# Score products of even and odd heads issued in alternation into two PSUM banks, and a compression in blocks of 64 columns

## The chip, the core and the metric

One core of a Trainium2 chip (trn2) runs the whole program. The metric is the device time of one execution in microseconds (us). Five engines matter: TensorE (PE; its weight loads are shown as PEld), VectorE (DVE), ScalarE (ACT), GpSimd (POOL) and SyncE (SP), which issues the transfers.

## What is computed

Two blocks of two layers each on x of 256 x 1024 in float32. A layer of the first block is FFN, mixer, FFN; one of the second is mixer, FFN. Only the mixers are touched. Cut to what matters:

```python
# first mixer: 12 dilated heads in 3 groups share one softmax per query; 4 stick-breaking heads
s = einsum('bhrnqd,bhrnkd->bhrnqk', qb, kw) * 64 ** -0.5
...
z = einsum('bhqd,bhkd->bhqk', q_blk, k) * 64 ** -0.5
...
# second mixer: keys are compressed in blocks of 32 at stride 16 by an MLP, for K and for V
blk = swapaxes(k[:, idx], 2, 3) + pos
k_cmp = gelu(blk.reshape(bsz, n_cmp, g, 32 * 64) @ w1) @ w2
...
# 8 query heads over 2 key heads: attention to the compressed keys,
# to selected blocks and to a window of 512 (at 256 positions both are plain causal attention),
# and a fourth branch with a window of 128 and a sink
s = einsum("bqgrd,bkgd->bgrqk", qb, kb) * 64 ** -0.5
```

Head size is 64 everywhere, so a score product contracts 64 rows.

## The kernel before, in words

The 256 positions are two tiles t = 0, 1 of 128 rows. Linear layers run on PE with each operand split into a high and a low part (type fp32r): three products per tile (`mm3`, lines 184 to 186, or `lin_T`, `lin_T2`), with weights that `chunk` (line 104) loads by SP, and ACT (line 110, `wh`) and DVE (line 111, `wl`) convert, six buffers deep. PSUM has 8 banks: a pool `lin` of 4 for linear products and a pool `aux` of 4 for everything else. A scheduler places the instructions of each engine in a fixed order from the priorities of the code; it mixes linear products in between the steps of the attentions.

`attend1` (line 398) is the attention of the first mixer. `QT[t]` holds q and k transposed, two heads on top of each other: even heads in partitions 0 to 63, odd ones in 64 to 127 (`qk`, line 421). For each j of 4 the three heads j, 4 + j, 8 + j (one per group, so all of one parity) get their mask by a product with the identity (line 434) and their scores (line 440) in one aux bank at t = 0 and two at t = 1; then follow the maximum (line 442), the exponential (451), transposes (`transposed`, line 152), the copy to SBUF and the products with v (468). The stick-breaking heads take one bank per parity (lines 477 and 483).

`attn` (line 525) is called three times per tile in the second mixer, once with a window and sinks and twice causal. `scores(h0)` takes 4 heads of one parity at t = 0, 2 at t = 1, in one bank: mask (538 to 542), scores (546), maximum (549), exponentials (558). `output` transposes and multiplies by v (572). At most AHEAD = 2 score groups wait for their output. All groups of even heads come first, then those of odd heads:

```python
        for par in range(2):
            for h0 in range(par, 8, 2 * per):
                ahead.append(scores(h0))
```

The scores against the compressed keys (line 829) also go parity by parity. In `compress` (line 704) 16 slices of the blocks are the held operand, 32 columns wide (15 blocks and one of zeros for each of 2 key heads), split into `ah` and `al`; three products per slice go into 32 rows of one aux bank `hps` (lines 723 to 725), 16 slices for K and 16 for V. After the last linear product that follows, `hr` takes the GELU (749), is transposed (752), copied (754), multiplied by w2 for K (757), copied four ways by POOL (764) and multiplied by w2 for V (768).

On DVE a convolution of 31 taps (lines 863 and 866, 120 steps of line 866 a layer) fills the gaps of the second mixer.

Of the kernel before, what the change touches and what calls it, by code (L numbers as in the profile page):

```python
# [25 lines left out]
def body(tc, ctx, I, C, out, upto=99):  # L26
# [371 lines left out]
    def attend1(qkn, vs):  # L398
        QT = [None, None]
        oTs = []  # L400
        for t in range(2):
# [26 lines left out]
            for j in range(4):  # L428
                groups = [[0, 1, 2]] if t == 0 else [[0, 1], [2]]
                ps_l, mx, sm = [], stat(4), stat(4)  # L430
                for gi, gs in enumerate(groups):
                    n = len(gs) * nk * P
                    ps = aux_ps()[:, :n]
                    nc.tensor.matmul(ps, identb, dilm[t][:, gs[0]:gs[-1] + 1, :].rearrange("p g k -> p (g k)"),
                                     start=True, stop=False)
# [6 lines left out]
                    V.tensor_reduce(mx[:, gi:gi + 1], ps, op=OP.max, axis=AX.X)  # L442
                    ps_l.append(ps)
# [26 lines left out]

            n = nk * 256
            e2 = big("b", "se")
            zs, es, ws = [], blocks2(e2, n), []
            for par in range(2):
                o = par * 64
                z = aux_ps()[:, :n]
                nc.tensor.matmul(z[:, n - 256:], identb, sbm[:, None, :].to_broadcast([P, 2, P]), start=True, stop=False)
                for kt in range(nk):
                    for jj in range(2):
# [3 lines left out]
                        nc.tensor.matmul(z[:, c0:c0 + P], k_, q_, start=False, stop=(kt == nk - 1 and jj == 1))  # L483
                S.activation(es[par], z, AF.Abs)
                zs.append(z)
# [39 lines left out]
    def attn(t, qT, kTf, vf, window, sink=None):  # L525
# [5 lines left out]
        def scores(h0):  # L531
            par = h0 % 2
            hs = list(range(h0, h0 + 2 * per, 2))
            n = per * nk * P
            ps = aux_ps()[:, :n]
            pv = ps.rearrange("p (h k) -> p h k", h=per)
            if t == 0:
                nc.tensor.matmul(pv, identb, swm[:, None, P:].to_broadcast([P, per, P]), start=True, stop=False)
            elif window:
                nc.tensor.matmul(pv, identb, swm[:, None, :].to_broadcast([P, per, 2 * P]), start=True, stop=False)  # L540
            else:
                nc.tensor.matmul(pv[:, :, P:], identb, swm[:, None, P:].to_broadcast([P, per, P]), start=True, stop=False)
# [5 lines left out]
            sl = slice(h0, h0 + 2 * per - 1, 2)  # L548
            V.tensor_reduce(mx[:, sl], pv, op=OP.max, axis=AX.X)
            if sink is None:  # L550
                V.tensor_scalar(ng[:, sl], mx[:, sl], -0.125, None, op0=OP.mult)
            else:
                V.scalar_tensor_tensor(mx[:, sl], mx[:, sl], 0.125, sink[:, sl], op0=OP.mult, op1=OP.max)
                V.tensor_scalar(ng[:, sl], mx[:, sl], -1.0, None, op0=OP.mult)
            e = unit("e")[:, :n]
            ev = e.rearrange("p (h k) -> p h k", h=per)
            for i, h in enumerate(hs):
# [597 lines left out]
```

## Time and profile before

| | |
|---|---|
| median of 3 runs | 2174.1 us (2173.64 to 2177.4) |
| the profiled execution | 2173.62 us, span 2171.8 us |
| PE busy | 2142.1 us, 99% |
| weight loads (PEld) busy | 1824.8 us, 84% |
| DVE busy | 1567.7 us, 72% |
| ACT busy | 1159.0 us, 53% |
| POOL busy | 38.7 us, 2% |
| granted TensorE clock, mean | 0.998 |

The busy time of PE is that of pipelined products with modelled ends: the duration of one is not what it costs. Each float32 product of two operands appears as two records, a transpose or an fp32r product as one.

### The profile page before, as it was taken

To read this page: it belongs to the slowest core of one execution; us is meant where nothing else is said; L and a number is where in the kernel's file an instruction comes from. 1 tells how busy PE (TensorE), PEld (TensorE's weight loads), DVE (VectorE), ACT (ScalarE), POOL (GpSimd) and SP (SyncE) were. 2 spreads that over 40 slices of the span, in tenths; PEclk is the share of its full clock that TensorE was granted. 3 is DMA by queue.
4 is the path that set the end of the run, shared out by engine and by line. 5 is a ranking of instruction groups with operands and counts; after the bars stand their busy time and mean duration, and the time that the engine had idled before them with its cause. 6 is when DMAs were issued, how large, how long until landed. Compare 5 with 4: busy or idle time off the path is not lost.

```text
span 2171.8 us, 30964 instructions
## 1 busy us (share of the span) xinstructions
PE 2142.1 (99%) x11824; PEld 1824.8 (84%) x11824; DVE 1567.7 (72%) x2395; ACT 1159.0 (53%) x1766; POOL 38.7 (2%) x55
## 2 busy tenths in 40 slices
PE   7999999999999999999999999999999999999998
PEld 6888888888888888888887888889987888888997
DVE  6875556786677555577757997678976898577983
ACT  5654545554555455555545554456655554446652
POOL 0000000000000000000000000000000000000000
PEclk9999999999999999999999999999999999999999
DMA  8666534666666654366666632456656643355653
GB/s 252 202 193 186 193 97 139 192 192 190 192 188 187 188 191 127 118 183 185 190 188 198 200 117 78 155 172 200 192 188 191 216 140 113 107 184 175 186 179 121
DMA packets 250821, 373.86 MB, mean 172 GB/s; under 512 B 14768, under 2 KB 123696, under 8 KB 250672
## 3 DMA queue, kind: packets, MB, share of 16 engines
q1 hardware_dynamic: 250096, 371.48, 55.8%
q8 instruction: 93, 1.52, 0.3%
q0 software_dynamic: 576, 0.39, 0.1%
q14 instruction: 56, 0.46, 0.1%
HBM read 371.17 MB, written 1.05 MB: 171 GB/s over the span
## 4 chain that ended last, share of the span: by engine, by line
PE 93%; DVE 3%; issue 1%; DMA 1%; ACT 1%; POOL 1%; SPq 0%; POOLq 0%; DVEq 0%; ACTq 0%
PE lin L186 17%; PE lin L184 17%; PE lin L185 16%; PE lin L218 15%; PE lin L219 8%; PE aux L155 4%; PE lin L206 3%; PE lin L205 3%; PE lin L204 3%; PE aux L546 2%; PE aux L572 1%; DVE wl L111 1%; PE aux L440 1%; PE aux L468 1%; ACT wh L110 0%
## 5 line engine op out<-in xcount | busy, mean ns | idle before, releaser
L111 DVE TENSOR_TENSOR wl<-raw,wh 128x1024 fp32r<-128x1024 f32 (+1 forms) x688 | 835.1, 1217 | 407.5 <-ACT wh L110 399.8
L110 ACT ACTIVATE wh<-raw 128x1024 fp32r<-128x1024 f32 (+1 forms) x688 | 723.2, 1055 | 557.0 <-PE lin L186 314.1
L218 PE MATMUL lin<-x,wh 128*128 128x512 f32 x1408 | 494.9, 396 | 0.0
L219 PE MATMUL lin<-x,wl 128*128 128x256 f32 x1408 | 395.3, 281 | 0.0
L184 PE MATMUL lin<-wh,x 128*128 128x512 f32 (+2 forms) x896 | 350.0, 391 | 0.0
L185 PE MATMUL lin<-wl,x 128*128 128x512 f32 (+2 forms) x896 | 348.2, 389 | 1.5 <-DVE wl L111 1.5
L186 PE MATMUL lin<-wh,x 128*128 128x512 f32 (+2 forms) x896 | 348.2, 389 | 1.0 <-DVE rs L1057 0.8
L218 PEld LDWEIGHTS lin<-x,wh 128*128 128x128 f32 x1408 | 264.5, 188 | 61.6
L219 PEld LDWEIGHTS lin<-x,wl 128*128 128x128 f32 x1408 | 266.4, 189 | 0.5 <-DVE wl L111 0.4
L186 PEld LDWEIGHTS lin<-wh,x 128*128 128x128 f32 x896 | 168.9, 189 | 34.5 <-DVE rs L1057 1.6
L185 PEld LDWEIGHTS lin<-wl,x 128*128 128x128 f32 x896 | 168.9, 189 | 33.0 <-DVE wl L111 1.9
L184 PEld LDWEIGHTS lin<-wh,x 128*128 128x128 f32 x896 | 168.8, 189 | 32.6 <-ACT wh L110 0.4
L186 PE MATMUL lin<-wh,lo 128*128 128x512 f32 x480 | 188.6, 393 | 0.4 <-DVE lo L147 0.4
L184 PE MATMUL lin<-wh,hi 128*128 128x512 f32 x480 | 187.2, 390 | 0.0
L185 PE MATMUL lin<-wl,hi 128*128 128x512 f32 x480 | 187.0, 390 | 0.0
L205 PE MATMUL lin<-x,wh 128*128 128x256 f32 x576 | 163.2, 283 | 0.0
L206 PE MATMUL lin<-x,wl 128*128 128x256 f32 x576 | 163.0, 283 | 0.0
L204 PE MATMUL lin<-x,wh 128*128 128x256 f32 x576 | 163.0, 283 | 0.0
L205 PEld LDWEIGHTS lin<-x,wh 128*128 128x128 f32 x576 | 110.6, 192 | 0.1
L204 PEld LDWEIGHTS lin<-x,wh 128*128 128x128 f32 x576 | 110.6, 192 | 0.1
L206 PEld LDWEIGHTS lin<-x,wl 128*128 128x128 f32 x576 | 110.6, 192 | 0.0
L186 PEld LDWEIGHTS lin<-wh,lo 128*128 128x128 f32 x480 | 90.1, 188 | 19.5 <-DVE lo L147 1.3
(317 smaller groups left out, 2774.0 us busy)
## 6 DMA issues: line engine op xcount, KB each, us to landing
raw<-in_ffn_w_up_dram SPq DMA_DIRECT2D x168, 512.0 KB, 4.3
raw<-in_ffn_w_down_dram SPq DMA_DIRECT2D x132, 512.0 KB, 4.2
raw<-in_w_in_dram SPq DMA_DIRECT2D x132, 512.0 KB, 4.1
raw<-in_ffn_w_gate_dram SPq DMA_DIRECT2D x88, 512.0 KB, 4.4
raw<-in_w_gate_dram SPq DMA_DIRECT2D x64, 512.0 KB, 3.8
raw<-in_w_branch_dram SPq DMA_DIRECT2D x32, 512.0 KB, 4.4
raw<-in_w_out_dram SPq DMA_DIRECT2D x16, 512.0 KB, 4.4
raw<-in_nsa_cmp_w_dram SPq DMA_DIRECT2D x16, 512.0 KB, 4.3
```

What stands on the lines that cost most here:

```text
L110: S.activation(wh, raw, AF.Copy)
L111: V.tensor_sub(wl, raw, wh.bitcast(F32))
L155: nc.tensor.transpose(p[:, i * P:(i + 1) * P], s, ident)
L184: nc.tensor.matmul(ps, xt.h[k], w[0], start=start, stop=False)
L185: nc.tensor.matmul(ps, xt.h[k], w[1], start=False, stop=False)
L186: nc.tensor.matmul(ps, xt.l[k], w[0], start=False, stop=stop)
L204: nc.tensor.matmul(o, wh, xh, start=k == 0 and i % 2 == 0, stop=False)
L205: nc.tensor.matmul(o, wh, xl, start=False, stop=False)
L206: nc.tensor.matmul(o, wl, xh, start=False, stop=k == 7 and i % 2 == 1)
L218: nc.tensor.matmul(o, wh, x, start=k == 0, stop=False)
L219: nc.tensor.matmul(o[:, :T], wl, x[:, :T], start=False, stop=k == 7)
L546: nc.tensor.matmul(pv[:, i, kt * P:(kt + 1) * P], q_, kTf(kt, h), start=False, stop=(i == per - 1 and kt == nk - 1))
```

## The change

Everywhere that scores of even and odd heads were computed one parity after the other, a step now takes two groups of opposite parity, with a bank of its own for each, and issues their products in turn. `attend1` takes j = 0 and 1 together, then 2 and 3:

```diff
-            for j in range(4):
-                groups = [[0, 1, 2]] if t == 0 else [[0, 1], [2]]
-                ps_l, mx, sm = [], stat(4), stat(4)
+            def scores(js):
+                r = [([], stat(4), stat(4)) for _ in js]
                 for gi, gs in enumerate(groups):
                     n = len(gs) * nk * P
-                    ps = aux_ps()[:, :n]
...
+                    pss = [aux_ps()[:, :n] for _ in js]
+                    for ps in pss:
+                        nc.tensor.matmul(ps, identb, dilm[t][:, gs[0]:gs[-1] + 1, :].rearrange("p g k -> p (g k)"),
+                                         start=True, stop=False)
                     for gg in gs:
-                        h = gg * 4 + j
                         for kt in range(nk):
                             c0 = ((gg - gs[0]) * nk + kt) * P
-                            nc.tensor.matmul(ps[:, c0:c0 + P], qk(h, False, t), qk(h, True, kt), start=False,
-                                             stop=(gg == gs[-1] and kt == nk - 1))
+                            for ps, j in zip(pss, js):
+                                h = gg * 4 + j
+                                nc.tensor.matmul(ps[:, c0:c0 + P], qk(h, False, t), qk(h, True, kt), start=False,
+                                                 stop=(gg == gs[-1] and kt == nk - 1))
...
+            for js in ((0, 1), (2, 3)):
+                for j, r in zip(js, scores(js)):
+                    output(j, *r)
```

The stick-breaking scores and those against the compressed keys are turned round in the same way. In `attn` one call of `scores` makes both parities, and the loop over groups follows:

```diff
-            for i, h in enumerate(hs):
-                q_ = qT[par * 64:par * 64 + 64, (h // 2) * P:(h // 2 + 1) * P]
+            for i in range(per):
                 for kt in range(nk):
-                    nc.tensor.matmul(pv[:, i, kt * P:(kt + 1) * P], q_, kTf(kt, h), start=False,
-                                     stop=(i == per - 1 and kt == nk - 1))
+                    for par, pv in enumerate(pvs):
+                        h = h0 + 2 * i + par
+                        q_ = qT[par * 64:par * 64 + 64, (h // 2) * P:(h // 2 + 1) * P]
+                        nc.tensor.matmul(pv[:, i, kt * P:(kt + 1) * P], q_, kTf(kt, h), start=False,
+                                         stop=(i == per - 1 and kt == nk - 1))
...
-        for par in range(2):
-            for h0 in range(par, 8, 2 * per):
-                ahead.append(scores(h0))
-                if po is None:
-                    po = aux_ps()
-                if len(ahead) > AHEAD:
-                    output(*ahead.pop(0))
+        for h0 in range(0, 8, 2 * per):
+            ahead += scores(h0)
+            if po is None:
+                po = aux_ps()
+            while len(ahead) > AHEAD:
+                output(*ahead.pop(0))
```

The compression holds the high and the low part of a slice side by side, 64 columns, and needs two products: rows 0 to 31 of the result hold what the high part gives, rows 32 to 63 what the low part gives (this adds the product of the two low parts). They are added after the transpose, the GELU comes behind that, and the four copies of POOL become four GELUs on ACT. All this stands after the rotary step of the first tile instead of before both:

```diff
-            ah, al = unit("cAh", F32R), unit("cAl", F32R)
-            split(A, ah, al)
+            ahl = []
+            for q in range(2):
+                x = unit("cAh", F32R)
+                v = x.rearrange("p (s a n) -> p s a n", s=8, a=2)
+                split(A[:, q * 256:(q + 1) * 256].rearrange("p (s n) -> p s n", s=8), v[:, :, 0], v[:, :, 1])
+                ahl += [x[:, i * 64:(i + 1) * 64] for i in range(8)]
...
-                    nc.tensor.matmul(o, ah[:, a], ws[i][0], start=s == 0, stop=False)
-                    nc.tensor.matmul(o, ah[:, a], ws[i][1], start=False, stop=False)
-                    nc.tensor.matmul(o, al[:, a], ws[i][0], start=False, stop=s == 15)
+                    nc.tensor.matmul(o, ahl[s], ws[i][0], start=s == 0, stop=False)
+                    nc.tensor.matmul(o, ahl[s], ws[i][1], start=False, stop=s == 15)
...
-        hr = unit("hr")[0:32, :]
-        S.activation(hr, hps, AF.Gelu_apprx_tanh)
...
+                S.activation(hg4, h4[:, :, 1], AF.Copy)
+                V.tensor_tensor(hg4, h4[:, :, 0], hg4, op=OP.add)
+                hk = hg[:, 0:64]
...
+                        S.activation(hv5[:, hf, a], hg[:, 64 + hf * 32:96 + hf * 32].rearrange("p (g n) -> p g n", g=2)
+                                     [:, :, None, :].to_broadcast([P, 2, 2, 16]), AF.Gelu_apprx_tanh)
+                S.activation(hk, hk, AF.Gelu_apprx_tanh)
```

How this moves PE's instructions is seen in three places. A row is line, operation, written tile, read tiles and shape; `aux_` with a number is one tile of the aux pool. First the causal attention of the second mixer at t = 1, before:

```order
L542 LDWEIGHTS identb
L542 MATMUL aux_11449<-swm,identb 128x2x128
L546 MATMUL aux_11449<-kT_10823,qT_11408 128x128
L546 MATMUL aux_11449<-kT_10843,qT_11408 128x128
L546 MATMUL aux_11449<-kT_10823,qT_11408 128x128
L546 MATMUL aux_11449<-kT_10843,qT_11408 128x128
L542 LDWEIGHTS identb
L542 MATMUL aux_11461<-swm,identb 128x2x128
L546 MATMUL aux_11461<-kT_10823,qT_11408 128x128
```

And the same place now:

```order
L556 MATMUL aux_11446<-swm,identb 128x2x128
L556 LDWEIGHTS identb
L556 MATMUL aux_11448<-swm,identb 128x2x128
L563 MATMUL aux_11446<-kT_10773,qT_11382 128x128
L563 MATMUL aux_11448<-kT_10773,qT_11382 128x128
...
L563 MATMUL aux_11448<-kT_10809,qT_11382 128x128
L184 MATMUL lin_12038<-wh_12016,x_9761 128x512
L185 MATMUL lin_12038<-wl_12017,x_9761 128x512
L186 MATMUL lin_12038<-wh_12016,x_9761 128x512
L155 MATMUL aux_11468<-ident,e_11437 128x128 x4
```

Groups of 4 products into one bank have become runs of 8 that change the bank with every product; three linear products stand between the second such run and the first transpose of the exponentials.

Second the first mixer at t = 1, where a pair of heads takes four aux tiles, now:

```order
L444 MATMUL aux_2553<-qt_2523,qt_2522 128x128
L444 MATMUL aux_2554<-qt_2523,qt_2522 128x128
L437 LDWEIGHTS identb
L437 MATMUL aux_2567<-dilm_86,identb 128x256
L437 LDWEIGHTS identb
L437 MATMUL aux_2568<-dilm_86,identb 128x256
L444 MATMUL aux_2567<-qt_2357,qt_2522 128x128
L444 MATMUL aux_2568<-qt_2357,qt_2522 128x128
L444 MATMUL aux_2567<-qt_2523,qt_2522 128x128
L444 MATMUL aux_2568<-qt_2523,qt_2522 128x128
L185 MATMUL lin_2892<-wl_2845,x_1607 128x512
```

Nine linear products follow before the transposes of the exponentials; before the change a single head's two tiles stood there.

Third the place behind the compression, before:

```order
L752 MATMUL aux_10793<-ident,hr_10791 128x32 x4
L184 MATMUL lin_10878<-wh_10856,x_9761 128x512
L185 MATMUL lin_10878<-wl_10857,x_9761 128x512
...
L184 MATMUL lin_10878<-wh_10862,x_9761 128x512
L757 MATMUL aux_10800<-hg_10798,w_10472 128x32 x2
L768 MATMUL aux_10809<-w_10472,hv_10804 128x64 x2
L185 MATMUL lin_10878<-wl_10863,x_9761 128x512
```

And now, from the transposes of hr on (20 linear products, all but one left out here, follow them):

```order
L786 MATMUL aux_10786<-ident,hr_10784 128x64 x4
L186 MATMUL lin_10852<-wh_10842,x_9996 128x512
...
L155 MATMUL aux_10810<-ident,kd_10800 128x128 x4
L155 MATMUL aux_10816<-ident,dd_10801 128x128 x2
L804 MATMUL aux_10820<-hg_10791,w_10472 128x32 x2
L809 MATMUL aux_10824<-w_10472,hv_10792 128x64 x2
```

The two small products stood 7 linear products behind the transposes of hr, one behind the other; now they stand 20 linear products and six transposes behind them.

## Rows read from the trace of the kernel before

**Rows 1.** The page: span; busy time of PE; shares of the last chain by engine.
```profile
span 2171.8 us, 30964 instructions
...
PE 2142.1 (99%) x11824; PEld 1824.8 (84%) x11824; DVE 1567.7 (72%) x2395; ACT 1159.0 (53%) x1766; POOL 38.7 (2%) x55
...
PE 93%; DVE 3%; issue 1%; DMA 1%; ACT 1%; POOL 1%; SPq 0%; POOLq 0%; DVEq 0%; ACTq 0%
```

**Rows 2.** Groups of PE by form: line, tiles, shape, count | busy us, mean ns | idle before.
```profile
L572 PE MATMUL aux<-vv,pt 128*128 128x64 f32 x288 | 36.1, 270 | 0.0
L546 PE MATMUL aux<-kT,qT 64*128 64x128 f32 x192 | 28.8, 287 | 0.0
```

**Rows 3.** Timeline of PE in the first mixer: start us, us, instruction, count.
```profile
333.52 0.71 PE L483 MATMUL aux<-qt,qt 64*128 64x128 f32 x4
334.16 0.66 PE L468 MATMUL aux<-v,pt 128*128 128x64 f32 x4
...
335.60 0.71 PE L483 MATMUL aux<-qt,qt 64*128 64x128 f32 x4
336.15 0.61 PE L483 MATMUL aux<-qt 64*128 64x128 f32 x4
336.69 0.50 PE L185 MATMUL lin<-wl,x 128*128 128x512 f32 x1
```

**Rows 4.** Timeline of PE, window attention of the second mixer, t = 0.
```profile
1246.38 0.40 PE L186 MATMUL lin<-wh,x 128*128 128x512 f32 x1
...
1246.70 1.71 PE L546 MATMUL aux<-dkT,qT 64*128 64x128 f32 x16
...
1248.34 0.50 PE L184 MATMUL lin<-wh,x 128*128 128x512 f32 x1
...
1248.68 0.40 PE L185 MATMUL lin<-wl,x 128*128 128x512 f32 x1
...
1248.91 0.40 PE L186 MATMUL lin<-wh,x 128*128 128x512 f32 x1
```

**Rows 5.** Timeline of PE, compression and the linear products behind it.
```profile
1195.26 0.28 PE L723 MATMUL aux<-wh,cAh 128*32 128x256 f32 x1
...
1197.64 0.28 PE L184 MATMUL lin<-wh,x 128*128 128x256 f32 x1
...
1197.99 0.28 PE L184 MATMUL lin<-wh,x 128*128 128x256 f32 x1
```

**Rows 6.** Waits of PE (total us, times, longest), and groups of ACT, behind the compression.
```profile
PE aux L768 <- POOL hv L764: 2.3, 2, 1.3
...
PE aux L757 <- ACT hg L754: 0.6, 1, 0.6
...
L749 ACT ACT_TABLE_LOAD x1 | 1.3, 1283 | 0.0
...
L749 ACT ACTIVATE hr<-aux 32x512 f32<-32x512 f32 x2 | 1.2, 580 | 0.0
```

**Rows 7.** Timeline of PE behind these waits, and a window: busy us, PEclk, DMA.
```profile
1220.05 0.63 PE L186 MATMUL lin<-wh,x 128*128 128x512 f32 x1
1220.48 0.63 PE L184 MATMUL lin<-wh,x 128*128 128x512 f32 x1
...
1218.00:1221.50 3.50, 3.50 (x10) 2.74 (x9) 3.50 (x8) 0.00 (x0) 0.00 (x0) 0.52 0.69 256
```

**Rows 8.** Groups of DVE and ACT by form: maximum and exponentials at t = 1.
```profile
L549 DVE TENSOR_REDUCE st<-aux 128x2 f32<-128x512 f32 x24 | 16.5, 689 | 8.7 <-PE aux L546 8.5
...
L558 ACT ACTIVATE e<-aux,st 128x256 f32<-128x256 f32 x48 | 22.2, 471 | 30.5 <-DVE st L551 18.3 <-PE aux L155 7.0 <-DVE st L553 5.3
...
L558 ACT ACTIVATION_READ_ACCUMULATOR e<-aux,st 128x1 f32 x96 | 19.7, 206 | 0.0
```

**Rows 9.** A window (us; busy PE, PEld, DVE, ACT, POOL), and a group of DVE.
```profile
1188.70:1245.20 56.50, 54.57 (x333) 47.68 (x333) 52.75 (x99) 31.66 (x46) 2.21 (x4) 0.97 0.68 208
...
L866 DVE SCALAR_TENSOR_TENSOR cy<-cT,pm,cy 128x251 f32<-128x251 f32 (+17 forms) x240 | 101.4, 462 | 0.2
```

More of the change, by code (lines that the diff above doesn't have):

```diff
@@ L482, in attend1 @@
                         c0 = kt * 256 + jj * P
-                        nc.tensor.matmul(z[:, c0:c0 + P], k_, q_, start=False, stop=(kt == nk - 1 and jj == 1))
-                S.activation(es[par], z, AF.Abs)
-                zs.append(z)
+                        nc.tensor.matmul(zs[par][:, c0:c0 + P], k_, q_, start=False, stop=(kt == nk - 1 and jj == 1))
+            for par in range(2):
+                S.activation(es[par], zs[par], AF.Abs)
             S.activation(e2[:, :2 * n], e2[:, :2 * n], AF.Exp, scale=-1.0)
@@ L531, in scores @@
         def scores(h0):
-            par = h0 % 2
-            hs = list(range(h0, h0 + 2 * per, 2))
             n = per * nk * P
[L535 to L542, printed above, removed]
@@ L555, in scores @@
-            e = unit("e")[:, :n]
-            ev = e.rearrange("p (h k) -> p h k", h=per)
-            for i, h in enumerate(hs):
-                S.activation(ev[:, i], pv[:, i], AF.Exp, bias=ng[:, h:h + 1], scale=0.125, accum_out=dn[:, h:h + 1])
-            return h0, e
+            pvs = []
+            for _ in range(2):
+                pv = aux_ps()[:, :n].rearrange("p (h k) -> p h k", h=per)
+                if t == 0:
+                    nc.tensor.matmul(pv, identb, swm[:, None, P:].to_broadcast([P, per, P]), start=True, stop=False)
+                elif window:
+                    nc.tensor.matmul(pv, identb, swm[:, None, :].to_broadcast([P, per, 2 * P]), start=True, stop=False)
+                else:
+                    nc.tensor.matmul(pv[:, :, P:], identb, swm[:, None, P:].to_broadcast([P, per, P]), start=True, stop=False)
+                pvs.append(pv)
@@ L561, in output @@
+            return r
         def output(h0, e):
@@ L780, in mixer2 @@
             V.tensor_copy(dkT[:, t * 256:(t + 1) * 256], transposed(blocks(dd, 2)))
+            if t == 0:
+                hr = unit("hr")[0:64, :]
+                S.activation(hr, hps, AF.Copy)
+                hp = aux_ps()[:, :256]
+                for i in range(4):
+                    nc.tensor.transpose(hp[:, i * 64:(i + 1) * 64], hr[:, i * P:(i + 1) * P], ident[0:64, 0:64])
+                h4 = hp.rearrange("p (i a n) -> p i a n", i=4, a=2)
+                hg, hv = unit("hg")[:, :128], unit("hv")[:, :256]
+                hg4 = hg.rearrange("p (i n) -> p i n", i=4)
+                S.activation(hg4, h4[:, :, 1], AF.Copy)
+                V.tensor_tensor(hg4, h4[:, :, 0], hg4, op=OP.add)
+                hk = hg[:, 0:64]
+                hv5 = hv.rearrange("p (f a g r n) -> p f a g r n", f=2, a=2, g=2, r=2)
+                for hf in range(2):
+                    for a in range(2):
+                        S.activation(hv5[:, hf, a], hg[:, 64 + hf * 32:96 + hf * 32].rearrange("p (g n) -> p g n", g=2)
+                                     [:, :, None, :].to_broadcast([P, 2, 2, 16]), AF.Gelu_apprx_tanh)
+                S.activation(hk, hk, AF.Gelu_apprx_tanh)
+        kps = aux_ps()
+        for hf in range(2):
+            nc.tensor.matmul(kps[:, 0:32], w2k[:, hf].rearrange("p a d -> p (a d)"), hk[:, hf * 32:hf * 32 + 32],
+                             start=hf == 0, stop=hf == 1)
+        S.activation(kcT, kps[:, 0:32], AF.Copy)
+        vps = aux_ps()[:, :64]
+        for hf in range(2):
+            nc.tensor.matmul(vps, hv[:, hf * P:(hf + 1) * P], w2v[:, hf], start=hf == 0, stop=hf == 1)
+        V.tensor_tensor(h8(vblk), vps[:, None, :].to_broadcast([P, 8, 64]), bc(hsel), op=OP.mult)
         for name, c0, lst in (("qd", 1304, qd),):
```

70 lines of the change are left out of this document (31 added, 39 removed).

## The prediction

> **What bounds the kernel now.** I read the page first: TensorE (PE) is busy in 2142.1 of 2171.8 us, and the chain that ended last is 93% PE [rows 1]. So what leaves PE's stream shortens the run, and what only makes another engine busier costs nothing until PE has to wait for it. A matmul's duration in the groups is a latency (272 ns for a score product), and matmuls are pipelined; what one costs is the distance from its start to the next start, so I took prices from the timeline of PE.
>
> The groups give the counts: 96 score products of the two causal attentions per layer are 192 records [rows 2], two for each float32 product. By the loops all score products are 72 (dilated), 24 (stick-breaking), 144 (three attentions of the second mixer) and 32 (compressed keys): 272, or 544 records. Their operands have 64 rows; even heads lie in rows 0 to 63, odd heads in 64 to 127.
>
> In mixer1 a run of 4 score records of one parity takes 0.64 us up to the next start, a run of 8 takes 1.09 us [rows 3]. The 4 more cost 0.45, so a record costs 0.112 us and a run has a fixed 0.19. The product ahead of a run is longer too: 0.32 us where such a product takes 0.23 [rows 4], 0.09 more. PE thus pays 0.28 us each time it goes from 128-row to 64-row products and back, and 0.112 per record.
>
> One kind of run is shorter than that. In the window attention at t = 0, four even heads (8 records) are followed by four odd ones (8 records), into another bank. These 16 take 1.64 us [rows 4]; at 0.112 each it would be 1.98. Three records cost nothing: records of the other parity were at work at the same time. This is the overlap that the change asks for everywhere, and the trace of before has it in 8 runs only.
>
> **The change, part by part.** *Score products.* The order lists show 72 runs of score products before, nearly all of one parity, and 40 now, each strictly alternating between two banks. Before: 544 x 0.112 + 72 x 0.28 - 8 x 0.34 (the overlap there is) = 60.9 + 20.2 - 2.7 = 78.4 us. Now, if each pair costs what one did: 272 x 0.112 + 40 x 0.28 = 30.5 + 11.2 = 41.7. **Gain 36.7 us.** Bounds: with no overlap at all 6.2 remain (only the switches fall), and more than a full overlap there isn't. I take the full one, since in [rows 4] the overlapped records cost nothing.
>
> *Compression.* It was three products for each of 16 slices, twice a layer: 192 at 0.113 us ((1197.64 - 1195.26) / 21 [rows 5]). It is now two with 64 columns held: 64 fewer, 7.2 us. The held block doubles; with 128 columns held the same 256 columns take 0.117 ((1197.99 - 1197.64) / 3 [rows 5]), so the 128 left lose 0 to 0.5. **Gain 7.0.**
>
> *What follows the compression.* PE waited 0.6 us for ACT and 2.3 us for POOL there, in both layers together [rows 6]. In the first layer the clock then fell: right after these waits the granted clock was 0.52 for 3.5 us (the 1.2 GHz level), and a product of 0.23 us took 0.43 [rows 7]: 8 products, 1.6 us lost. The change takes POOL out, and puts 20 linear products (4.6 us) and two sets of transposes between the transposes of hr and their use. In that time ACT has a table load (1.28 us) and five small activations, which cost less than the 0.58 of the larger one there was [rows 6]: at most 4.2. The wait is covered, and were it not, its end would be late by some tenths. **Gain 4.5.** The kcT and vblk tiles are late by the same amount, but their first use (the compressed scores) comes after the whole window attention.
>
> *Added elsewhere.* Splitting in two halves and one add to join the 32-row halves: about 1 us more of DVE and ACT a layer, beside PE. The number of table loads stays 14.
>
> *New waits.* This is the term that the trace can't price, because PE waited for nothing in the attention stages of before. Three places. (a) A pair of score tiles is followed by fewer PE instructions before the first transpose of the exponentials. In the causal attention at t = 1, first step: 8 more products with their seeds (about 1.6 us), then 3 linear ones (0.7), 2.3 in all; in that time DVE must reduce (0.69) and ACT take two exponentials with their accumulator reads (2 x 0.68) [rows 8], 2.1 with nothing queued ahead. Cover and chain are equal. (b) At t = 1 in mixer1 a pair of heads fills all four aux banks, and 9 linear products (2.1) stand before the first transpose, for a chain with one more reduction than before. (c) From the compression to the window attention DVE was busy 52.8 of 56.5 us [rows 9]. The PE time of that stretch falls by some 8 us, to 48.5. The order list moves 11 convolution steps (0.46 each [rows 9]) behind it, which leaves DVE 47.7 and the extra 0.6: as full as PE. From below nothing; from above I take 0.6 us for each of the 30 places where a softmax follows a pair, and 2 us a layer for DVE: 22. I choose **5.5**, near the lower end: with chains as close to their cover in before, PE's idle time for the lines of scores and outputs was 0.0 [rows 2].
>
> **Sum.** Profiled execution 2173.6 us (span 2171.8, and 1.8 around it; 0.5 under the median of the runs, 2174.1): 2173.6 - 36.7 - 7.0 - 4.5 + 5.5 = **2131 us**. A difference of 0.2% (4.3 us) is about what a measurement of this kernel can tell from none.
>
> **Rivals.**
> 1. *Softmax chains and DVE come late* (a, b and c at the upper end). For it: the four aux banks are full, DVE is at 93% [rows 9]. Against: the conversion of weights runs ahead, and nothing waited so far. 8 to 20 us more than no wait: 2139 to 2148. The Trainium skill, TensorEngine Tiling (Array Packing), section Performance Considerations, says that packing speeds up TensorE and not the emptying of PSUM, which may become the bottleneck. That is this rival's mechanism; so far the rows agree with it only in that the chain is as long as its cover [rows 8].
> 2. *Records start strictly in order.* Then the second record of an even product must start before the odd product can, and each run needs one record's time more: 40 x 0.112 = 4.5, 2135. Against: in the run of 16 such an order would let one record overlap (1.87 us), and it took 1.64 [rows 4]. The Trainium skill, TensorE: Matmul & The Clock Gate, Part 3, states this rule (matmuls start and end in program order); the run of 16 speaks against it.
> 3. *No overlap in the alternating order*, because what overlapped in [rows 4] were records at the seam of two long groups. PE would pay 272 x 0.112 = 30.5 more: 2161.
> 4. *Slower.* The aux banks: with two tiles held per step, every transpose waits for a whole chain, because no bank comes free earlier. Price 2.2 us (as worked out under a) at 30 places: 66, 2173.6 - 48.2 + 66 = 2191. It decides from 1.75 us a place on (52.5 / 30). Against it stand the 3 to 15 linear products that the order list keeps behind nearly every pair.
> 5. *It does not do what it says*: the order would not alternate. The order list excludes that.
>
> **Chances.** Forecast (2124 to 2139) 0.62; rival 1 0.17; rival 2 0.08; rival 3 0.06; between rival 1 and no gain 0.04; rival 4 0.03. The range reaches from the sum without any new wait (2125), with another 2 us for stages that shift against the clock, to the end of rival 1: 2123 to 2148; rivals 3 and 4 lie outside. Faster by over 0.2%: 0.95; within: 0.02; slower: 0.03, which is rival 4.
>
> **What would show it.** A run of 8 score products (16 records) should last about 1.09 us up to the next start, in the dilated, window and causal attentions alike; 1.98 would mean rival 3, 1.2 rival 2. Between the transposes of hr and the two small matmuls there should be no wait, and no POOL at all; the 1.2 GHz stretch behind them should be gone. Compression records: 128, 0.113 to 0.117 apart. PE's idle time at the transposes of the exponentials should be some tenths of a microsecond a place; if it is over one, rivals 1 and 4 are at work, and the releaser (ACT e, DVE, or a bank) says which.

## The result, and the profile after

The changed kernel takes 2142.12 us (median of 4 runs, 2138.39 to 2148.56), the kernel before 2175.75 us on the same chip (4 runs): the ratio is 0.9843, with a 95% interval of 0.9809 to 0.9877. A second set of runs gave 2140.00 against 2174.6 us, ratio 0.9844 (0.9831 to 0.9858). The forecast was 2131, with a range of 2123 to 2148. The profiled execution took 2143.28 us, 30.3 less than the one before.

From the page after, to be held against [rows 1]:

```profile
span 2141.5 us, 30861 instructions
...
PE 2105.3 (98%) x11757; PEld 1788.2 (84%) x11760; DVE 1564.6 (73%) x2401; ACT 1159.7 (54%) x1780; POOL 34.2 (2%) x47
...
PE 90%; DVE 6%; DMA 1%; ACT 1%; issue 1%; POOL 1%; SPq 0%; DVEq 0%; ACTq 0%; POOLq 0%
```

PE still sets the end, but its share of the chain fell from 93% to 90% and DVE's rose from 3% to 6%: new waits.

**What left PE.** Timeline of PE after, causal attention at t = 1 (one pair of score groups, masks, the next pair), and the first and last compression product of V:

```profile
1312.40 1.16 PE L563 MATMUL aux<-kT,qT 64*128 64x128 f32 x16
1313.49 0.39 PE L556 MATMUL aux<-swm,identb 128*128 128x256 bf16 x2
...
1186.31 0.28 PE L747 MATMUL aux<-wh,cAh 128*64 128x256 f32 x1
...
1189.84 0.28 PE L748 MATMUL aux<-wl,cAh 128*64 128x256 f32 x1
```

Sixteen records now take 1.09 us up to the next start, where the run of 16 in [rows 4] took 1.64. The records of a pair start 6 to 7 ns apart and the next pair 105 ns later, 0.112 us a pair. Over all runs of score records (worked out from their starts) 72 runs of 71.2 us became 40 of 38.0. The 32 compression records are (1189.84 - 1186.31) / 31 = 0.114 us apart, as before [rows 5]; 64 held columns cost no more than 32, and with 64 records fewer their sum fell from 22.0 to 14.6 us.

**What came instead.** Waits of PE in the second mixer of the first layer, after (total us, times, longest):

```profile
PE aux L155 <- DVE kd L537: 2.5, 1, 2.5
PE aux L155 <- ACT e L578: 2.3, 3, 1.0
PE lin L185 <- DVE wl L111: 1.0, 2, 0.8
PE aux L917 <- POOL st L914: 0.5, 1, 0.5
PE aux L155 <- DVE qr L537: 0.2, 1, 0.2
```

Two of these rows are old: 0.76 us of the wait for `wl` stood there before too, and so did the one for `st` (0.46). The waits for POOL hv and ACT hg in [rows 6] are gone. The transposes of the rotated keys (`kd`) and of the exponentials (`e`) wait now. [rows 2] shows the rows of scores and outputs; the wait is at the transposes between them. Groups of PE, PE's idle time last, for `e` before, then for `e` and `kd` after:

```profile
L155 PE MATMUL aux<-ident,e 128*128 128x128 f32 x216 | 37.5, 277 | 0.2
```

```profile
L155 PE MATMUL aux<-ident,e 128*128 128x128 f32 x216 | 36.3, 279 | 4.5 <-ACT e L578 4.5
...
L155 PE MATMUL aux<-ident,kd 128*128 128x128 f32 x16 | 2.5, 279 | 4.3 <-DVE kd L537 4.3
```

Measured from start to start beyond the usual distance, `kd` costs 2.71 and 1.91 us in the two layers, and `e` 0.65, 0.99 and 1.14 us in the first, 0.65, 0.99 and 1.14 in the second.

*How kd comes late.* Timeline after around 1190 us: PE (the last product of the first tile's key columns; the kd transposes), ACT, DVE, and the window's row with DMA share and GB/s at its end:

```profile
1192.94 0.29 PE L186 MATMUL lin<-wh,x 128*128 128x280 f32 x1
...
1200.10 0.66 PE L155 MATMUL aux<-ident,kd 128*128 128x128 f32 x4 [2.54 <-DVE kd L537]
...
1194.46 1.06 ACT L110 ACTIVATE wh<-raw 128x1024 fp32r<-128x1024 f32 x1 [2.99 <-DMA raw<-in_w_in_dram]
1195.79 1.06 ACT L110 ACTIVATE wh<-raw 128x1024 fp32r<-128x1024 f32 x1 [0.27 <-DMA raw<-in_w_in_dram]
1196.75 0.35 ACT L763 ACTIVATE kk<-lin,rs 128x128 f32<-128x128 f32 x1
...
1195.55 1.23 DVE L111 TENSOR_TENSOR wl<-raw,wh 128x1024 fp32r<-128x1024 f32 x1 [1.74 <-ACT wh L110]
...
1197.13 0.56 DVE L529 TENSOR_TENSOR ra<-kk,rope 128x384 f32<-128x384 f32 x1
...
1198.23 1.22 DVE L111 TENSOR_TENSOR wl<-raw,wh 128x1024 fp32r<-128x1024 f32 x1
1199.36 0.68 DVE L537 TENSOR_TENSOR kd<-ra,rb 128x512 f32<-128x512 f32 x1
...
1188.00:1196.00 8.00, 8.00 (x66) 8.00 (x65) 6.19 (x13) 3.50 (x6) 0.00 (x0) 1.00 0.94 316
```

The key columns of the first tile were complete about 1193.2, yet ACT copied them (`kk`) only at 1196.75. Ahead of the copy in ACT's queue stand two conversions of the *next* weights, and the first of them waited 2.99 us for its transfer. Then the chain on DVE (`ra`, `rb`, `kd`) runs at once, but with one more conversion (1.22 us) inside it. From 1188 to 1196 the transfers were nearly full: 94% busy, 316 GB/s. PE is done with 6.4 MB of weights (by their sizes in the kernel) from the first compression product to the last key column in 16.0 us now (1180.05 to 1196.04, 400 GB/s), where before it took 20.5 (1191.33 to 1211.84, 312 GB/s): a 512 KB chunk of compression weights lasts for 8 records now instead of 12.

Bandwidth is not all of it. From 1180 to 1188 the transfers were only 66% busy (199 GB/s), because SP issued no load of weights between 1179.57 and 1184.01: all four raw buffers were taken, and DVE began to convert the next of them only at 1182.76. Waits of SP from 1175 to 1195:

```profile
SPq L107 <- DVE wl L111: 7.6, 5, 4.0
```

*How e comes late.* Timeline of DVE, ACT and PE after, the causal attention at t = 1 that begins with the scores shown above:

```profile
1313.04 1.22 DVE L111 TENSOR_TENSOR wl<-raw,wh 128x1024 fp32r<-128x1024 f32 x1
1314.17 1.28 DVE L569 TENSOR_REDUCE st<-aux 128x2 f32<-128x512 f32 x2
1315.37 0.16 DVE L571 TENSOR_SCALAR st<-st 128x2 f32<-128x2 f32 x1
...
1315.62 0.47 ACT L578 ACTIVATE e<-aux,st 128x256 f32<-128x256 f32 x1 [3.34 <-DVE st L571]
...
1315.48 0.40 PE L186 MATMUL lin<-wh,x 128*128 128x512 f32 x1
1316.69 0.66 PE L155 MATMUL aux<-ident,e 128*128 128x128 f32 x4 [0.82 <-ACT e L578]
```

The first pair was done at about 1313.5. DVE was in a weight conversion, then reduced both banks, and only then came the small scaling (L571) that the first exponential needs. The chain took 3.2 us, its cover (the second pair and three linear products) 2.2.

### The profile page after: what moved, and what is told of

Read it like the earlier page. It is cut to its first block, busy times and chain, and to the rows that moved or that the text cites. A ratio compares the mean times of both kernels' runs of the same rounds, so it can differ in the third digit from the quotient of the medians.

```text
span 2141.5 us, 30861 instructions
## 1 busy us (share of the span) xinstructions
PE 2105.3 (98%) x11757; PEld 1788.2 (84%) x11760; DVE 1564.6 (73%) x2401; ACT 1159.7 (54%) x1780; POOL 34.2 (2%) x47
## 4 chain that ended last, share of the span: by engine, by line
PE 90%; DVE 6%; DMA 1%; ACT 1%; issue 1%; POOL 1%; SPq 0%; DVEq 0%; ACTq 0%; POOLq 0%
PE lin L186 16%; PE lin L185 16%; PE lin L184 16%; PE lin L218 15%; PE lin L219 8%; PE aux L155 4%; PE lin L206 3%; PE lin L205 3%; PE lin L204 3%; DVE wl L111 2%; PE aux L593 2%; DVE cy L897 1%; DMA raw<-in_w_in_dram 1%; PE aux L476 1%; ACT wh L110 1%
## 5 line engine op out<-in xcount | busy, mean ns | idle before, releaser
L225 ACT ACTIVATE su<-lin 128x256 f32<-128x256 f32 x176 | 65.2, 374 | 79.7 <-PE lin L219 79.7
```

The lines of the kernel that those rows point to most:

```text
L225: S.activation(u[:, i * T:(i + 1) * T], p[:, T:], AF.Copy)
```

## The experiments

The theory after the first look: the gains are as computed, and the change loses about 15 us to chains that are late at PE, each half of the change bringing its own. The rivals differ from set to set and stand in the expectations. Each set was run beside its own runs of the kernel before. "Rest" is the time from the last product of the fourth FFN to the end, from the profiles: 1096.6 before, 1078.7 after. It leaves out a scatter of the FFNs that is told of at the end.

**Each half alone.** The first is the kernel before with the alternating scores, the second with the new compression.

> The alternating scores with the compression of before. Theory A (each part of the change has its own losses: the scores lose about 4 us a layer of the second mixer, because the exponentials come late out of DVE's queue, and the compression loses its own elsewhere): gain 36.6 of the overlap less 8 us of waits, about 2147 us (2144 to 2150) where before is 2175.5; waits of PE for ACT's exponentials 2.5 to 3 us a layer as in the changed kernel, no wait for kd, the old waits for POOL and hg (3.4 us in both layers) still there. Rival B (the 18 us that the whole change lost all come with the overlapped scores, wherever they show): about 2157 us. Rival C (the losses in the scores come only because the new compression makes PE earlier everywhere): no waits at the exponentials, about 2139 us.

2144.65 us (2141.84 to 2151.3), before 2176.13; ratio 0.9857 (0.9840 to 0.9874). Theory A: the waits for `e` are there with the old compression (2.6 us in the first layer), no wait for `kd`, the old ones for POOL and hg still are.

> The new compression with the scores of before. Theory A (the compression brings its own loss, a wait for the rotated keys kd of 2.7 and 1.9 us and 1 to 2 us of waits for wl): gain 7.5 (64 records a run of the kernel fewer) and 4.8 (old waits and the 1.2 GHz stretch), loss about 6: 2169 to 2170 us where before is 2175.5, with the kd wait in the trace at both layers. Rival C (the kd wait needs the faster scores of the first mixer or chance): no kd wait, about 2163 us.

2169.66 us (2167.19 to 2174.23), ratio 0.9971 (0.9958 to 0.9983). Theory A again: PE waits 2.64 and 1.36 us for `kd`, although no score was touched. So each half brings its own wait.

**Is the alternation itself needed?** Same pairs of banks, one parity after the other:

```diff
-            for i in range(per):
-                for kt in range(nk):
-                    for par, pv in enumerate(pvs):
+            for par, pv in enumerate(pvs):
+                for i in range(per):
+                    for kt in range(nk):
```

> The changed kernel with the same pairs of banks, but in each pair all products of the even heads first, then all of the odd ones. Theory A (only products of the other parity that are neighbours in the queue overlap, as in the run of 16 of before, where three records were free): a run of 8 products takes 1.6 us instead of 1.09, in all 272 x 0.112 - 40 x 0.34 = 17 us more, less up to 3 us because the reduction of the even heads can start half a run earlier: 2156 to 2159 us. Rival D (PE looks further ahead in its queue than three records, and the alternation in code is not needed): 2142 us, a run of 16 records near 1.1 us. Rival E (pairing without alternation gives nothing at all beside the fewer switches): 272 x 0.112 = 30 us more, 2172 us.

2154.40 us (2153.03 to 2155.67), ratio 0.9899 (0.9884 to 0.9914). Its timeline of PE:

```profile
1330.66 1.71 PE L563 MATMUL aux<-kT,qT 64*128 64x128 f32 x16
1332.31 0.39 PE L556 MATMUL aux<-swm,identb 128*128 128x256 bf16 x2
```

The run of 16 takes 1.65 us as in [rows 4]; of its starts, three lie 4 to 6 ns behind another, at the seam. The score runs sum to 54.7 us instead of 38.0, 16.8 more. But no transpose of exponentials waits more than 0.13 us here: the first bank is complete half a run earlier. 16.8 less the 5.6 us of those waits is 11.2; by the ratios to the kernel before (0.9899 against 0.9843 and 0.9844) it is 12 us. The alternation pays 17 us and gives back a third of it in waits.

**Place or supply? The wait for kd.** First the block of hr was put ahead of the rotary steps, so that 24 linear products more stand ahead of the kd transposes.

```diff
+        hr = unit("hr")[0:64, :]
+        S.activation(hr, hps, AF.Copy)
...
         for t in range(2):
             kd, dd = unit("kd"), unit("dd")[:, :256]
...
-            if t == 0:
-                hr = unit("hr")[0:64, :]
...
```

> The changed kernel, with the block of hr (copy, transposes, GELUs) again ahead of the rotary step of the first tile, so that PE has the kd transposes 24 linear products (5.5 us) later. Theory A1 (the kd wait is a matter of place: 3 linear products behind the last product of the key columns, too few for the chain kk, ra, rb, kd): the waits for kd (4.6 us in both layers) go, nothing takes their place, 2142 less 4 to 5 is about 2137.5 us. Rival A2 (supply: the new compression takes 0.9 us of PE for a chunk of weights that costs DVE 1.22 us to convert and a transfer of 512 KB, so PE has used up the lead of the weights and has to wait for something): the wait for kd goes, but PE waits 3 us or more in both layers together for wl or wh in the linear products that now stand there, 2140 to 2142 us.

2140.34 us (2139.33 to 2141.22), ratio 0.9833 (0.9819 to 0.9846), rest 1074.7. With 5.5 us more of cover PE still waits 0.83 + 0.74 us in the first layer and 1.80 + 0.21 in the second. That is 1 us less, not 4.6: place alone is not it. Rival A2 misses too, for the wait for `kd` did not go; the waits for `wl` at the key columns are 0.6 and 0.7 us in the two layers.

The changed kernel once more, beside the next ones:

> The changed kernel once more, beside the others of this set. Two things of its first profile are taken here for chance: the first FFN lasted 126.35 us instead of 123.25 (each pair of products 353 ns instead of 347, in code that did not change), and a stretch at 1.2 GHz stood behind the wait for POOL's st in both layers of the second mixer instead of one. Theory: median 2140 to 2143 us; waits for kd 2.7 and 1.9 and for the exponentials 2.8 a layer come back within 0.2 us, while the FFN's 126.3 or 123.3 and the 1.2 GHz stretches are drawn anew. Rival: they belong to the change and come back the same.

2140.00 us (2139.14 to 2142.24). The waits for `kd` are 2.39 and 2.49, those for `e` the same to 0.01 us. What I took for chance was drawn anew (see the end).

The next two edits take the convolution out of DVE's queue, the first by leaving out 29 of its 31 taps:

> The changed kernel without 29 of the 31 taps of the convolution (two remain), so that DVE loses 116 steps of 0.46 us a layer. Theory D1 (DVE's queue: conversions of weights and convolution steps stand in front of the kd chain and of the reductions and scalings of the softmax): the waits for kd fall from 2.7 and 1.9 to under 1 us each, those for the exponentials from 2.8 to 1 to 2 us a layer; 2142 - 3 - 2 is about 2137 us. Rival D2 (supply: transfers of weights come too late behind the shorter compression, DVE would be free): waits for kd stay over 1.5 us or turn into waits for wl of the same size, 2140 to 2142 us. Rival D3 (PSUM banks hold up the transposes of the exponentials): their waits stay at 2.8 a layer.

```diff
-                for j in range(29, -1, -1):
+                for j in range(29, 28, -1):
```

2141.68 us (2137.16 to 2143.32), ratio 0.9845 (0.9832 to 0.9859). D2 for `kd`: 1.89 and 2.66 us, no less, with hardly a convolution step left. ACT and DVE in its timeline:

```profile
1193.92 1.06 ACT L110 ACTIVATE wh<-raw 128x1024 fp32r<-128x1024 f32 x1 [1.97 <-DMA raw<-in_w_in_dram]
...
1195.01 2.50 DVE L111 TENSOR_TENSOR wl<-raw,wh 128x1024 fp32r<-128x1024 f32 x2 [1.90 <-ACT wh L110]
```

ACT waits for the transfer and DVE idles behind it. For `e` it is D1 in part: the waits at causal t = 1 fall from 0.99 and 1.14 to 0.67 and 0.56, the one in the window attention stays at 0.65. In the first of these two places no conversion stands ahead of the reductions in this kernel either. DVE begins as soon as PE is done, and the chain still takes 2.65 us, longer than its cover (DVE, then PE, in its timeline):

```profile
1306.67 1.29 DVE L569 TENSOR_REDUCE st<-aux 128x2 f32<-128x512 f32 x2 [0.61 <-PE aux L563]
...
1309.22 0.66 PE L155 MATMUL aux<-ident,e 128*128 128x128 f32 x4 [0.51 <-ACT e L578]
```

So what is queued ahead is only part of that wait; both reductions, the scaling and two exponentials by themselves are the rest.

The second edit keeps the convolution and holds it back:

```diff
+        cbl = stat(4)
+        V.scalar_tensor_tensor(cbl, kd[:, 0:4], 0.0, cb, op0=OP.mult, op1=OP.add)
         kps = aux_ps()
...
-                V.tensor_scalar(y4[:, c], c4[:, c], cw[:, 30 * 4 + c:30 * 4 + c + 1], cb[:, c:c + 1], op0=OP.mult, op1=OP.add)
+                V.tensor_scalar(y4[:, c], c4[:, c], cw[:, 30 * 4 + c:30 * 4 + c + 1], cbl[:, c:c + 1], op0=OP.mult, op1=OP.add)
```

> hr again ahead of the rotary steps, and the first convolution step made to depend on kd of the second tile, so that no convolution step stands in DVE's queue ahead of the two kd chains; nothing is left out. Theory D1 (those steps, about 10 of 0.46 us, are what made kd late): the waits for kd, 3.6 us in both layers with hr ahead alone, fall under 1 us, waits for wl do not grow: 2140.3 - 3 is about 2137.5 us. Rival D2 (supply): waits for kd or wl of 3 us in both layers remain, 2140 us. Rival D4: the convolution, which starts some 5 us later, ends too late and PE waits for its result at the mean product: 2140 to 2145 us.

2141.32 us (2140.17 to 2142.86), ratio 0.9847 (0.9834 to 0.9861). D1 falls here too: `kd` still costs 1.14 + 0.35 and 1.37 + 0.18 us. No convolution step stands ahead of the chain now, but conversions do: between the copy of `kk` (complete at 1198.6) and the first step of the chain (1202.81) DVE spends 3.5 us on them.

Then the supply was changed, first by a load more:

```diff
         compress(1)
+        dm = big("g", "dm")
+        V.tensor_copy(dm[:, 0:1], kk[0][:, 256:257])
+        nc.sync.dma_start(dm.rearrange("p (s n) -> p s n", s=4), I["nsa_cmp_w1_2"][l, 1].rearrange("(s p) n -> p s n", p=P)[:, 0:4])
```

> The changed kernel with one more transfer of 512 KB a layer, into a tile that nobody reads, in SP's queue between the four loads of 280 columns and the loads of the next 512 columns; apart from that only one DVE step of one column is added. Theory D2 (supply: behind the shorter compression the loads follow each other without a gap, 1.6 us apart, and the next weights come late; DVE's queue holds their conversion ahead of the kd chain): everything behind it comes 1.3 to 1.6 us later, the waits for kd rise from 2.4 (2.7 and 2.5, 1.9 in the four places seen) to about 4 us, time 2140 to 2142 plus 3: 2143 to 2145 us. Rival D5 (only the place and DVE's own steps count): waits for kd unchanged, 2140 to 2142 us.

2143.95 us (2141.82 to 2146.94), ratio 0.9857 (0.9840 to 0.9873), rest 1080.0, which is 1.3 to 1.9 more than in the two profiles of the changed kernel. Not as I put it: the wait for `kd` did not grow, it became a wait for the weights themselves at the product ahead of it:

```profile
1197.85 1.06 ACT L110 ACTIVATE wh<-raw 128x1024 fp32r<-128x1024 f32 x1 [3.95 <-DMA raw<-in_w_in_dram]
1198.82 0.35 ACT L766 ACTIVATE kk<-lin,rs 128x128 f32<-128x128 f32 x1
...
1201.57 0.57 PE L185 MATMUL lin<-wl,x 128*128 128x512 f32 x1 [2.10 <-DVE wl L111]
```

ACT waits 0.96 us longer than in the changed kernel, and the copy of `kk` stands right behind that conversion. PE stands still for about the same time whichever of the two it needs first: 2.38 and 1.81 us for `wl`, where `kd` had cost 2.71 and 1.91. So one load more did not lengthen the wait, and the time is within the intervals of the changed kernel; what the run shows is the copy behind a late conversion once more.

Then by more room for loads:

```diff
-    rawp = ctx.enter_context(tc.tile_pool(name="rawp", bufs=4))
-    wp = ctx.enter_context(tc.tile_pool(name="wp", bufs=6))
+    rawp = ctx.enter_context(tc.tile_pool(name="rawp", bufs=6))
+    wp = ctx.enter_context(tc.tile_pool(name="wp", bufs=5))
```

> The changed kernel with six buffers for raw weights instead of four and five pairs of converted ones instead of six, the same memory. SP, which has no raw buffer free from about 1180 to 1184 us, can issue two loads more. Theory D2: the weights behind the compression come up to 3 us earlier, the waits for kd fall from about 2.4 to 1 us or less, waits for wl there vanish; 2140 - 3 is about 2137 us, if five converted pairs are enough everywhere. Rival D5: waits for kd stay at 2 us or more. Rival D6 (five converted pairs are too few): new waits for wl or wh all over the linear products, over 2142 us.

2141.48 us (2140.20 to 2141.67), ratio 0.9847 (0.9833 to 0.9862). The waits for `kd` fall to 0.35 and 0.36 us, as D2 has it. But in each layer PE now waits 1.88 us for `wh` and 1.27 for `wl` ahead of the compression, where it was 0.92 for `wl`: D6, in one place, takes it back. Nor are the buffers all that changed. The scheduler put 21 more products of 256 columns between the compression products, and a stretch at 1.2 GHz stands there in both layers (PEclk third from the end):

```profile
1176.90:1180.30 3.40, 3.40 (x19) 3.40 (x18) 2.80 (x10) 1.78 (x3) 0.00 (x0) 0.50 0.65 203
```

So the stage from the first compression product to the last key column lasts 20.0 us here, about as long as before, instead of 16.0.

And by both edits, this one and hr ahead:

> Six raw buffers and five converted pairs, and hr ahead of the rotary steps, so that the kd transposes stand 25 linear products later. Theory D2 (supply and place together make the wait): no wait for kd over 0.5 us, 2135 to 2137 us, faster than the changed kernel. Rival D5: waits for kd of 0.7 to 1.8 us as with hr ahead alone, 2139 to 2140 us.

2140.52 us (2139.78 to 2141.21), ratio 0.9844 (0.9830 to 0.9859). No wait for `kd` over 0.21 us, and the same two waits ahead of the compression. ACT in its timeline, where the copy no longer stands behind anything:

```profile
1195.89 0.37 ACT L763 ACTIVATE kk<-lin,rs 128x128 f32<-128x128 f32 x1 [1.69 <-PE lin L186]
```

How late the copy of `kk` for the first tile was (from the end of its last product, both layers), and what PE then waited for that tile's `kd`:

| kernel | kk late by, us | wait for kd, us |
|---|---|---|
| before | 0.75, 0.04 | 0, 0 |
| scores alone | 0.91, 0.04 | 0, 0 |
| compression alone | 2.94, 1.62 | 2.64, 1.36 |
| changed | 3.52, 2.21 | 2.71, 1.91 |
| changed, again | 2.69, 2.77 | 2.39, 2.49 |
| two taps | 2.22, 2.98 | 1.89, 2.66 |
| six raw buffers | 0.04, 0.04 | 0.35, 0.36 |
| six raw, hr ahead | 0.04, 0.04 | 0, 0 |

Every kernel with the new compression and four raw buffers has the copy 1.4 us late or more (those left out here too), with the old compression or six raw buffers it is 0.9 at most. The stage lasts 16.0 to 17.4 us in the first group and 19.8 to 20.7 in the second. So a late copy goes with a short stage; what six buffers would do in a stage of 16 us was not run.

**The wait for e: the scaling on ACT.**

```diff
-                    V.tensor_scalar(ng[:, sl], mx[:, sl], -0.125, None, op0=OP.mult)
+                    S.activation(ng[:, sl], mx[:, sl], AF.Copy, scale=-0.125)
```

> The changed kernel with the scaling of the maximum by -0.125 on ACT instead of DVE in the four causal attentions of both layers. Theory D1 (the exponentials wait for this small step because it stands in DVE's queue behind the second reduction, 0.64 us, and sometimes a convolution step, 0.46): from the start of the first score product of causal attention t = 1 to the first transpose of its exponentials it is 4.3 us now and 3.5 to 3.8 then. The order keeps 2 linear products fewer in that gap, 0.46 us, so that only 0.1 to 0.5 us a place comes back: 2140 to 2142 us. Rival D3 (banks): still 4.3 us, and the time rises to 2143 or more because 8 ACT steps of 0.2 us are added.

2141.20 us (2139.45 to 2142.78), ratio 0.9846 (0.9833 to 0.9860): nothing gained. From the first score product to the first transpose of exponentials it is 4.06 us in the one causal attention at t = 1 and 3.50 in the other, after 4.29 and 4.21, so the step on DVE was part of the chain. In the first, a mask product also waited 0.49 us for a bank. The scheduler put fewer linear products into the gap, and PE still waits 0.75 and 1.09 us, where the changed kernel has 0.99 and 1.14. Banks alone (D3) would have left the gap at 4.3.

**A version that uses this.** hr ahead as above, and:

```diff
-    rawp = ctx.enter_context(tc.tile_pool(name="rawp", bufs=4))
+    rawp = ctx.enter_context(tc.tile_pool(name="rawp", bufs=5))
...
-        return act.tile([P, cols], dt, tag="u", name=nm(name), bufs=18)
+        return act.tile([P, cols], dt, tag="u", name=nm(name), bufs=15)
```

> hr ahead of the rotary steps, five buffers for raw weights and still six converted pairs; the memory comes from the small work tiles (15 instead of 18). Theory D2 (one load more can be under way, 1.6 us of supply): the waits for kd, 3.6 us in both layers with hr ahead alone, fall to 1 us or less, and the waits of 1.9 and 1.3 us for wh and wl that five converted pairs brought ahead of the compression do not come back. From the second block's first attention input to the end it is 2 to 3 us less than with hr ahead alone; in the median 2137 to 2139 us, since an FFN by chance still takes 2 to 3 us more or less. Rival D7 (15 work tiles are too few, or another stage takes the time back): 2140 us or more, with waits of PE for work tiles or new waits in the attentions.

2136.79 us (2134.40 to 2142.78), before 2173.67; ratio 0.983 (0.9814 to 0.9846), rest 1074.4. The waits ahead of the compression do not come back, but `kd` still costs 1.62 and 2.04 us: the forecast for the time held, its reason did not. The rest, which was to fall by 2 to 3 us, is that of hr ahead alone (1074.7). It is the fastest median, 3 and 5 us under the two sets of the changed kernel, but the intervals of the ratios overlap (0.9831 to 0.9858 for the second set), so a gain over the changed kernel is not shown.

## Why the prediction was right in sign and 11 us off

Sum of the terms, for the profiled execution:

| term | predicted | measured |
|---|---|---|
| scores | -36.7 | -36.3: runs 71.2 to 38.0, and 32 entries fewer of 0.095 |
| compression | -7.0 | -7.4: 22.0 to 14.6 |
| waits behind it, 1.2 GHz stretch | -4.5 | -4.8: waits 0.81, 1.45, 1.15; seven products of 0.2 more |
| new waits | +5.5 | +18.2: what remains to -30.3 |

- **The scores** hold to 1%. Most of the 0.4 us is one price: the 64 records against the compressed keys are 16 columns wide, and a run of 16 took 1.47 us before and takes 1.00 now, not 1.64 and 1.09. Rivals 2 and 3 are out: a run of 16 takes 1.09 us, not 1.2 or 1.98. The overlap does not come from seams of long groups but from neighbours in the queue.
- **The compression** holds, and nothing was lost to 64 held columns.
- **What follows the compression** holds: no POOL, no wait between the transposes of hr and the small products.
- **New waits is the step that failed.** I chose 5.5, "near the lower end", because PE had not waited before. Of the 18.2 us, 5.6 are at the exponentials, 4.6 at `kd` and 1.0 at `wl` just ahead of it; 3.1 are a slower first FFN, bad luck, for the same kernel also ran without it; 1.6 are a new stretch at 1.2 GHz, whose place changes from one execution to the next; the remaining 2.3 lie in places of 0.4 us or less. In the second profile, with the FFN at its short time, the span is 33.8 us shorter than before, and new waits come to 14.7.
  - Place (a), the causal attention at t = 1: the place was right, the chain was not. I counted 2.1 us "with nothing queued ahead"; with a weight conversion and both reductions in DVE's queue ahead of the scaling it is 3.2, and 2.65 where no conversion stood there.
  - Place (b), the first mixer: nothing over 0.2 us.
  - Place (c), from the compression to the window attention: the stretch was right, the cause only in part. I put it down to a full DVE. With the convolution steps gone the wait stays; in the changed kernel the transfer is late, and the copy that `kd` needs is stuck behind a conversion in ACT's queue. DVE's share there is the conversions: one inside the chain, and those that keep the raw buffers from being filled again. How much of the lateness is bandwidth and how much is buffers was not taken apart. I had costed the shorter compression on PE alone and never asked whether its weights can come in 0.9 us a chunk instead of 1.36.
- **Rival 1** (2139 to 2148, chance 0.17) is what happened. Its range does not follow from its price: 8 to 20 us over no wait (2125) is 2133 to 2145; the measured time lies in both. Its softmax half is as described; in place of its full DVE stands, in the changed kernel, the late transfer. The Trainium skill, PSUM — Partial Sum Buffer, section Engine vs sequencer instructions, says that the queues of ScalarE, VectorE and GpSimdE are strictly first in, first out; the trace agrees, the copy of `kk` was 3.52 us late behind a conversion that waited 2.99 us for its transfer.

With hr ahead and five raw buffers the copies are only 1.78 and 1.08 us late, and yet `kd` waits. There it is the full DVE. Its first layer: the copy on ACT, then DVE, and a window's row, in which DVE's busy time is the third after the length:

```profile
1192.67 0.35 ACT L763 ACTIVATE kk<-lin,rs 128x128 f32<-128x128 f32 x1
...
1194.81 2.35 DVE L111 TENSOR_TENSOR wl<-raw,wh 128x1024 fp32r<-128x1024 f32 x2
...
1197.75 0.55 DVE L529 TENSOR_TENSOR ra<-kk,rope 128x384 f32<-128x384 f32 x1
...
1198.76 1.21 DVE L111 TENSOR_TENSOR wl<-raw,wh 128x1024 fp32r<-128x1024 f32 x1
1199.89 0.68 DVE L537 TENSOR_TENSOR kd<-ra,rb 128x512 f32<-128x512 f32 x1
...
1193.05:1200.50 7.45, 6.12 (x32) 4.72 (x30) 7.45 (x15) 7.25 (x16) 0.00 (x0) 1.00 0.90 310
```

DVE is busy in all of the 7.45 us: about 4.5 go to conversions of weights and 1.3 to three convolution steps. No run took the conversions away, so their part is read from the trace and not tested.

## What to carry to other kernels

Two float32 products that contract 64 rows each, in opposite halves of the rows and with a PSUM bank each, cost one here if they are neighbours in the order; grouped by half they overlap only at the seam. (Both into one bank was not tried.) Whoever makes a stage shorter on the engine that bounds the kernel should divide the bytes that it uses up by its new time. Here that came to 400 GB/s, above the 316 of nearly full transfers, and the wait showed up later, at a step that has nothing to do with weights but stands behind their conversion in an engine's queue. And a chain whose cover shrinks should be priced with everything that stands ahead of it in each queue: here 3.2 us and not 2.1.

## What the hardware showed that I had not expected

**Two rhythms of one and the same FFN.** The first FFN did not change, but took 123.25 us before, 126.35 after and 123.30 in the second profile of the changed kernel. It is not a wait but a steady pace: windows from 40 to 80 us (busy PE with its records first) before, after, and after again.

```profile
40.00:80.00 40.00, 40.00 (x233) 35.24 (x232) 34.16 (x47) 24.40 (x39) 0.00 (x0) 1.00 0.80 238
```

```profile
40.00:80.00 40.00, 40.00 (x229) 34.72 (x228) 33.37 (x45) 23.33 (x36) 0.00 (x0) 1.00 0.77 234
```

```profile
40.00:80.00 40.00, 40.00 (x233) 35.25 (x232) 33.90 (x46) 24.21 (x38) 0.00 (x0) 1.00 0.74 233
```

In this window a pair of products (512 and 256 columns) starts every 347 ns, or every 353 on average (two of three pairs after about 350, the third after 361), at full clock. In 14 profiles the first FFN lasted 122.7 to 123.7 us nine times and 125.5 to 126.4 five times, the second 123.6 nine times and 125.7 five times, the third and fourth always 125.5 to 125.8. That alone moves a run by up to 5 us. What decides between the two was not found.

**The same wait, sometimes with a slow stretch behind it.** PE waits 0.63 to 0.69 us for POOL's `st` in every profile. Shortly ahead of the wait stand 16 products of one column each, which take 1.8 us up to the next start; after, first layer:

```profile
1358.26 1.94 PE L910 MATMUL aux<-avg,sq 128*128 128x1 f32 x16
```

Windows after (behind `st`, first layer), and in its second profile (behind the 2.39 us for `kd`; behind `st`); PEclk is the third figure from the end.

```profile
1362.50:1365.50 3.00, 3.00 (x8) 2.32 (x8) 3.00 (x7) 1.21 (x2) 0.00 (x0) 0.50 0.00 0
```

```profile
1197.00:1200.30 3.30, 3.30 (x9) 2.57 (x9) 3.30 (x6) 2.91 (x4) 0.00 (x0) 0.50 0.87 274
1361.00:1364.00 3.00, 3.00 (x15) 2.48 (x14) 3.00 (x7) 2.12 (x3) 0.00 (x0) 1.00 0.03 6
```

At 1.2 GHz eight products take 0.2 us more each, 1.6 us. In the first profile this stood behind `st` in both layers and not behind `kd`, in the second behind `kd` in both layers and not behind `st`, with hr ahead behind neither.
